# Keeping back the next pair's weight copies in a macaron block: an order edge on ScalarE instead of two one-column writes on VectorE

## The chip, the cores and the metric

The kernel runs on one core of a Trainium2 chip. The core has TensorE (matmuls, PE in the profile, its weight loads PEld), VectorE (DVE), ScalarE (ACT), GpSimd (POOL) and SyncE (SP), which here issues nearly all DMAs. The metric is the device time of one execution in microseconds; the time of a kernel is the median of its runs.

## What is computed

One layer of a macaron block on 1024 frames of 1024 features in float32: half a SwiGLU feed-forward, a stick-breaking attention with 16 heads of 64, and half a second feed-forward, each behind an RMS norm.

```python
x = x + 0.5 * swiglu(rms_norm(x, n1), wi1, wo1)
x = x + stick_breaking_attention(rms_norm(x, gm), w_qkv, gq, gk, w_o)
x = x + 0.5 * swiglu(rms_norm(x, n2), wi2, wo2)

# attention, per head; q and k are RMS-normed per head
z = (q @ k.T) / 8                                # 1024 x 1024, only s < t counts
w[t, s] = sigmoid(z[t, s]) * prod(1 - sigmoid(z[t, j]) for s < j < t)
o = w @ v
```

## The kernel before

Every float32 matmul is made of three: each operand is split into a high part (a copy on ScalarE that rounds to the matmul's type, `hi`) and a low part (the difference, `lo`, by VectorE or GpSimd), and `mm3` (lines 301 to 310) adds hi·hi, hi·lo and lo·hi. `split` (lines 195 to 197) is that pair of instructions, so line 196 is always ScalarE's copy and line 197 the subtraction.

The two feed-forwards lie before and behind the attention stage. The attention stage works through eight pairs of heads, and the change lies there. In one round of 66 us the kernel scores one pair, applies its weights to the values, and computes q, k and v of the next pair. A round has four parts, a to d: the two heads times the two halves of the queries.

- **Scores** (`scores`, lines 1038 to 1073): two matmuls into a bank `bz` (L1058), two sigmoids on ScalarE (L1062; one gives the weight tile `w`, the other overwrites `bz` with 1 - sigmoid), a running product on VectorE (the scan, L1064, into `om` or `w`), and a multiply on GpSimd (L1071).
- **Values** (`values`, lines 1075 to 1130): transposes of `w` into a bank `bt` (L1093), the split into `th` (ScalarE, L196) and `tl` (VectorE, L197), and matmuls into a bank `bo`, first with `th`, then with `tl` (L1111). At the end of a head, `bo` is evacuated (L1116, L1117); the finished pair is split into `w` tiles (`w<-o`, L196 and L197) and stored by DMA (L1125).
- **Projections of the next pair** (`qkv`, lines 956 to 1010): 24 matmuls per block of 128 frames into a bank `bq`, in steps of nine, nine and six; then `bq` is evacuated by ScalarE (`sq`, `qk`, `vst`; L980, L981, L984). After four blocks VectorE computes the reciprocal roots (lines 208 to 212), the rates `r` (L992) and the factors `f` of the sigmoids (L1003), and GpSimd applies `r` to `qk` (L996, L999). `prep_q` and `prep_k` transpose them (L1016) and split them (L1020, L1021).
- **Weights of the pair after the next** (`weights_of`, lines 926 to 954): four steps, k = 0, 2, 4 and 6. Each loads two blocks of `w_qkv` by DMA into `raw_qkv` (L941, two tiles in turn), copies them on ScalarE into the high part `wqh` (L948), and GpSimd subtracts for the low part `wql` (L951). The four steps are put at fixed times of a round (`LOADS`, two in part c, two in part d).

What order the engines work in is decided when the program is built: a scheduler takes the instructions by the plan's order and by their dependencies and puts each engine's queue in order. A copy like L948 depends on its load alone, so it could be queued much earlier than the plan means. The kernel keeps it back by a small write: before the copy, an engine writes two columns (`[:, ks, 0]`, 128x2) of the tile that the copy will fill, from a value that is only known late (`behind`, L944 to L946). The copy overwrites that column, but it can't pass the write. In the rounds of pairs 2 to 7 the first two steps (k = 0 and 2) are held by a VectorE write of `r` into `wqh` and a GpSimd write of `qk` into `wql`; the last two by a GpSimd write into `wqh`.

There is a second means, used at line 947 for pair 1: `tc.issue_after(mark)` tells the scheduler to queue an instruction behind another one, without data between them. `following` (line 192) does the same and does nothing for `None`.

Of the kernel before, what the change touches and what calls it, by code (L numbers as in the profile page):

```python
# [12 lines left out]
AF = mybir.ActivationFunctionType  # L13
# [32 lines left out]
LOADS = (("c", 14.0), ("c", 15.0), ("d", 9.0), ("d", 10.0))  # L46
# [67 lines left out]
def macaron_kernel(ctx, tc, x, g1, w1_in, w1_out, gm, w_qkv, gq, gk, w_o, g2, w2_in, w2_out, out):  # L114
    nc = tc.nc
    act, dve, pool_e, pe, sp = nc.scalar, nc.vector, nc.gpsimd, nc.tensor, nc.sync
# [4 lines left out]
    marks = {}  # L121
# [70 lines left out]
    def following(mark):  # L192
        return tc.issue_after(mark) if mark is not None else nullcontext()
# [472 lines left out]
    with pools(*RAWS) as pr:  # L666
# [3 lines left out]
        with banks("ps1"), pools(*STREAM) as pa:  # L670
            with pools("x") as px, pools("xs", side="right") as pl:
                rows_of = {}

                def load_x(tbs):
# [5 lines left out]
                ss, mean, r = (  # L680
                    pl["xs"].tile([P, NT * n], F32, name=nm, bufs=1) for nm, n in (("ss", 2), ("mean", 1), ("r", 1))
                )
# [184 lines left out]
        with banks("ps2"), pools(*SECOND) as pl:  # L867
            lay_banks()
            gain_m = load_gain(pn, gm)
            half = pn["xs"].tile([P, 4, 2], F32, name="half", bufs=1)  # L870
# [45 lines left out]
    with ExitStack() as stack:  # L916
# [9 lines left out]
        def weights_of(p, state, behind, after=None):  # L926

            wh, wl = state["wq"] = {}, {}

            def step(n, k):
                if k % 4 == 0:
                    wq = pl[f"wq{(2 * p + k // 4) % 4}"]
                    state["h"], state["l"] = (wq.tile([P, 4, 3 * P], F32R, name=f"wq{n}", bufs=1) for n in "hl")
                h_, l_ = state["h"], state["l"]
                raw = pl["raw_qkv"].tile([P, 2, 3, P], F32, name="raw_qkv")
                src = w_qkv[k * P : (k + 2) * P, :].rearrange("(k p) (a c) -> p k a c", p=P, a=3)
                for i in range(2):  # L940
                    state["loaded"] = sp.dma_start(raw[:, i], src[:, i, :, p * P : (p + 1) * P]).ins  # L941
                ks = slice(k % 4, k % 4 + 2)
                raw = raw.rearrange("p k a c -> p k (a c)")
                for engine, to, f in behind[n]:  # L944
                    there = f().to_broadcast([P, 2])
                    engine.tensor_tensor((h_, l_)[to][:, ks, 0], there, there, op=ALU.mult)  # L946
                with tc.issue_after(after[k]) if after and k in after else nullcontext():
                    act.activation(h_[:, ks], raw, AF.Copy)  # L948
                for i in range(2):
                    k_ = k % 4 + i  # L950
                    pool_e.tensor_tensor(l_[:, k_, :], raw[:, i, :], h_[:, k_, :].bitcast(F32), op=ALU.subtract)  # L951
                    wh[k + i], wl[k + i] = h_[:, k % 4 + i, :], l_[:, k % 4 + i, :]

            return [partial(step, i // 2, k) for i, k in enumerate((4, 6, 0, 2) if p == 0 else (0, 2, 4, 6))]
# [83 lines left out]
        def scores(state, hd, half):  # L1038

            w = state["w", hd, half] = {}  # L1040

            def step(tb, kb):
                L = T - tb * P
                if kb == half:
                    t = pl["w"].tile([P, T - tb % 4 * P], F32, name=f"w{hd}{tb % 4}", bufs=1)

                    om = t[:, L : 2 * L] if half else pl["om"].tile([P, T], F32, name="om")
                    state["om"], w[tb] = om, t[:, :L]
                om, wt = state["om"], w[tb]
                q = state["q", hd, half][:, (tb % 4) * P : (tb % 4 + 1) * P]  # L1050
                s0 = max(tb * P, kb * NHALF)
                n = (kb + 1) * NHALF - s0
                c0 = s0 - tb * P
                off = P if n == P else 0
                z = bank("bz")
                keys = slice(s0 - off - kb * NHALF, NHALF)
                for i in range(2):
                    pe.matmul(z[:, : off + n], q, state["k", hd, kb][i][:, keys], start=i == 0, stop=i == 1)  # L1058

                z = z[:, off : off + n]  # L1060
                for to, sign in ((wt[:, c0 : c0 + n], 0), (z, 1)):
                    act.activation(to, z, AF.Sigmoid, scale=state["f", half][:, sign, tb % 4, hd : hd + 1])  # L1062
                least = first[:, P : P + 1].to_broadcast([P, n]) if c0 else first[:, :n]
                dve.tensor_tensor_scan(  # L1064
                    om[:, c0 : c0 + n], z, least, initial=om[:, c0 - 1 : c0] if c0 else 0.0,
                    op0=ALU.mult, op1=ALU.max,
                )
                if c0 == 0:
                    pool_e.memset(wt[:, 0:1], 0.0)
                c1 = max(c0, 1)  # L1070
                pool_e.tensor_tensor(wt[:, c1 : c0 + n], wt[:, c1 : c0 + n], om[:, c1 - 1 : c0 + n - 1], op=ALU.mult)  # L1071

            return [partial(step, tb, kb) for tb in range(half * 4, half * 4 + 4) for kb in range(half, 2)]

        def values(state, p, hd, half):
# [63 lines left out]
        states = [{} for _ in range(NP)]  # L1139
        plan = []  # L1140

        def spread(steps, t0, t1, at=0.5):
            plan.extend((t0 + (t1 - t0) * (i + at) / len(steps), f) for i, f in enumerate(steps))
# [9 lines left out]
                f()  # L1153
        first_q = ((pool_e, 0, lambda: states[0]["qk", 1][:, 0, 0, 0:1]),)
        evacuated = {}
        loads = weights_of(1, states[1], (first_q, first_q), evacuated)
        for i, f in enumerate(steps[:12]):
            f()

# [15 lines left out]
        for p in range(-1, NP):  # L1175
            this = states[p] if p >= 0 else None
            nxt = states[p + 1] if p < NP - 1 else None
            start, t = {}, PAIR * p
            for part, span in PARTS.items():
                start[part], t = t, t + span  # L1180

            def put(part, t, f):
                plan.append((start[part] + t, f))

            for part, span in PARTS.items():
                state = nxt if part == "d" else this
                if state is not None:
                    spread(scores(state, *UNITS[part]), start[part], start[part] + span, 0.5)
                if this is not None:
                    groups = values(this, p, *BEFORE[part])  # L1190
                    for i, (to_turn, to_apply) in enumerate(groups):
                        t = TURN + (span - TURN) * i / len(groups)
                        put(part, t, to_turn)
                        put(part, t + APPLY, to_apply)
            if nxt is not None:
                if p >= 0:
                    fills = qkv(p + 1, nxt)
                    for part, span in PARTS.items():
                        for i in range(FILLS[part]):
                            put(part, (span - (3.0 if part == "d" else 0.0)) * (i + 0.5) / FILLS[part], fills.pop(0))  # L1200
                put("c", 15.0, partial(prep_q, nxt, 1))
                put("c", 17.5 if p >= 0 else 20.0, partial(prep_k, nxt, 0, 1))
                put("d", 8.0, partial(prep_k, nxt, 1, 1))
            if this is not None:
                put("a", 5.0, partial(prep_q, this, 0))
                put("a", 7.5, partial(prep_k, this, 0, 0))
                put("b", 8.0, partial(prep_k, this, 1, 0))
            if 0 <= p < NP - 2:

                held = (  # L1210
                    ((dve, 0, lambda s=nxt: s["r"][:, 0, 0:1]), (pool_e, 1, lambda s=nxt: s["qk", 1][:, 0, 4, 0:1])),
                    ((pool_e, 0, lambda s=nxt: s["qk", 0][:, 2, 0, 0:1]),),
                )
                for at, f in zip(LOADS, weights_of(p + 2, states[p + 2], held)):
                    put(*at, f)
            if p == NP - 2:

                def note(i, f):
                    pool_e.tensor_tensor(seen[:, i : i + 1], f(), f(), op=ALU.mult)

                put("c", 14.0, partial(note, 0, lambda s=nxt: s["qk", 1][:, 0, 4, 0:1]))
                put("d", 1.0, partial(note, 1, lambda s=nxt: s["k", 0, 1][1][:, 0:1].bitcast(F32)))
                put("c", 10.0, partial(load_o, 1))
                put("d", 15.5, lambda: spots.append(tc.cur_priority))
            if p == NP - 1:
                put("a", 2.5, partial(load_o, 0))
                for at, _, _ in SHARES:
                    put(*at, lambda: spots.append(tc.cur_priority))
# [7 lines left out]
    after = ExitStack()  # L1236
# [128 lines left out]
```

## Time and profile before

| what | value |
|---|---|
| runs | 1933.4, 1935.77, 1935.79 us; median 1935.77 |
| profiled execution | 1933.84 us, its span 1932.1 us |
| clock granted to TensorE | full speed in all 40 slices |
| DMA | mean 134 GB/s over the span, about 40 GB/s in the attention rounds |
| VectorE writes at L946 | 12, from 739.9 to 1070.6 us |

The attention stage reaches from about 640 to 1250 us; its full rounds start at 740, 806, 872, 938 and 1004 us and so on. The page lists for each engine its busy time; the chain of waits goes back from the last instruction through whatever released it; the timeline gives single instructions with start and duration in us. A row's brackets hold the idle time of the engine ahead of it and what ended it. Times in the timeline count from the start of the span.

### The profile page before, as it was taken

To read this page: it belongs to the slowest core of one execution; us is meant where nothing else is said; L and a number is where in the kernel's file an instruction comes from. 1 tells how busy PE (TensorE), PEld (TensorE's weight loads), DVE (VectorE), ACT (ScalarE), POOL (GpSimd) and SP (SyncE) were. 2 spreads that over 40 slices of the span, in tenths; PEclk is the share of its full clock that TensorE was granted. 3 is DMA by queue.
4 is the path that set the end of the run, shared out by engine and by line. 5 is a ranking of instruction groups with operands and counts; after the bars stand their busy time and mean duration, and the time that the engine had idled before them with its cause. 6 is when DMAs were issued, how large, how long until landed. Compare 5 with 4: busy or idle time off the path is not lost.

```text
span 1932.1 us, 26665 instructions
## 1 busy us (share of the span) xinstructions
PE 1905.4 (99%) x9362; PEld 1622.9 (84%) x9362; DVE 1243.5 (64%) x1726; ACT 981.8 (51%) x1794; POOL 1115.5 (58%) x994
## 2 busy tenths in 40 slices
PE   9999999999999999999999999999999999999999
PEld 8878888888888898899889897788888888888887
DVE  6855455536775667887787778477555545548645
ACT  6433433444335467777787777344433443334332
POOL 6766667656456645555665664114667667654554
PEclk9999999999999999999999999999999999999999
DMA  6232323238896401111101144511323233369973
GB/s 202 93 120 99 104 88 126 95 123 305 315 341 233 134 17 49 35 39 45 44 31 47 50 135 149 194 57 53 122 88 125 95 102 102 122 216 340 334 264 142
DMA packets 169558, 259.70 MB, mean 134 GB/s; under 512 B 11728, under 2 KB 82384, under 8 KB 169424
## 3 DMA queue, kind: packets, MB, share of 16 engines
q1 hardware_dynamic: 169280, 258.00, 39.1%
q8 instruction: 73, 1.20, 0.3%
q14 instruction: 61, 0.50, 0.1%
q10 hardware_dynamic: 144, 0.00, 0.0%
HBM read 197.66 MB, written 60.29 MB: 134 GB/s over the span
## 4 chain that ended last, share of the span: by engine, by line
PE 84%; DVE 8%; ACT 3%; POOL 2%; issue 2%; DMA 1%; DVEq 0%; POOLq 0%; ACTq 0%
PE ka L308 6%; PE ka L309 6%; PE ka L310 6%; PE kc L309 4%; PE kc L308 4%; PE kc L310 4%; PE ma L310 4%; PE ma L308 4%; PE kb L309 4%; PE kb L308 4%; PE kb L310 4%; PE ma L309 4%; PE bq L308 4%; PE bq L309 4%; PE bq L310 4%; PE mb L310 3%
## 5 line engine op out<-in xcount | busy, mean ns | idle before, releaser
L197 POOL TENSOR_TENSOR rp<-raw,rp 128x1024 fp32r<-128x1024 f32 x84 | 210.2, 2507 | 172.6 <-ACT rp L196 157.0
L197 POOL TENSOR_TENSOR u<-sf,u 128x512 fp32r<-128x512 f32 x160 | 227.6, 1424 | 136.2 <-ACT u L196 136.2
L197 POOL TENSOR_TENSOR u<-raw,u 128x512 fp32r<-128x512 f32 x128 | 186.9, 1462 | 157.3 <-ACT u L196 156.5
L1071 POOL TENSOR_TENSOR w<-w,om 128x512 f32<-128x512 f32 (+4 forms) x128 | 141.1, 1106 | 114.7 <-DVE om L1064 88.5
L196 ACT ACTIVATE u<-sf 128x512 fp32r<-128x512 f32 x160 | 100.8, 630 | 204.7 <-PE kb L309 86.8
L446 DVE TENSOR_TENSOR h<-h 128x512 f32<-128x512 f32 x110 | 135.3, 1234 | 85.8 <-POOL h L554 85.1
L308 PE MATMUL bq<-wqh,xh 128*128 128x384 f32 x512 | 174.6, 341 | 0.0
L196 ACT ACTIVATE rp<-rh 128x1024 fp32r<-128x1024 f32 (+1 forms) x78 | 76.5, 984 | 189.9 <-issue 56.7
L310 PE MATMUL bq<-wqh,xl 128*128 128x384 f32 x512 | 172.2, 336 | 0.0
L309 PE MATMUL bq<-wql,xh 128*128 128x384 f32 x512 | 172.1, 336 | 0.0
L576 DVE TENSOR_TENSOR raw<-raw 128x1024 f32<-128x1024 f32 (+1 forms) x60 | 95.4, 1594 | 106.3 <-DMA raw<-w_out 95.5
L196 ACT ACTIVATE u<-raw 128x512 fp32r<-128x512 f32 x128 | 80.3, 630 | 151.5 <-PE ka L309 100.8
L308 PE MATMUL ka<-xh,u 128*128 128x512 f32 x352 | 137.2, 390 | 1.9 <-ACT s L499 1.9
L308 PE MATMUL ma<-rp 128*128 128x512 f32 x352 | 137.0, 389 | 0.0
L309 PE MATMUL ka<-xl,u 128*128 128x512 f32 x352 | 137.0, 389 | 0.0
L310 PE MATMUL ma<-rp 128*128 128x512 f32 x352 | 136.9, 389 | 0.0
L310 PE MATMUL ka<-xh,u 128*128 128x512 f32 x352 | 136.9, 389 | 0.0
L309 PE MATMUL ma<-rp 128*128 128x512 f32 x352 | 136.9, 389 | 0.0
L1062 ACT ACTIVATE w<-bz,f 128x512 f32<-128x512 f32 (+2 forms) x192 | 112.5, 586 | 40.5 <-PE bz L1058 39.0
L554 POOL TENSOR_TENSOR h<-h,g 128x512 f32<-128x512 f32 x80 | 113.0, 1412 | 34.9 <-DVE h L503 33.0
L475 DVE TENSOR_TENSOR sf<-raw 128x512 f32<-128x512 f32 x80 | 80.2, 1003 | 78.0 <-POOL u L197 78.0
L197 DVE TENSOR_TENSOR rp<-rh,rp 128x1024 fp32r<-128x1024 f32 (+1 forms) x70 | 107.7, 1555 | 22.2 <-ACT rp L196 19.6
(310 smaller groups left out, 5500.9 us busy)
## 6 DMA issues: line engine op xcount, KB each, us to landing
raw<-w_out SPq DMA_DIRECT2D x120, 512.0 KB, 5.5
raw<-w_in SPq DMA_DIRECT2D x86, 512.0 KB, 3.6
k<-h SPq DMA_DIRECT2D x154, 256.0 KB, 2.0
rh<-k SPq DMA_DIRECT2D x64, 512.0 KB, 6.2
raw_qkv<-w_qkv SPq DMA_DIRECT2D x64, 192.0 KB, 2.9
x_keep<-x SPq DMA_DIRECT2D x32, 256.0 KB, 3.7
x<-x_keep SPq DMA_DIRECT2D x32, 256.0 KB, 5.6
raw<-w_out SPq DMA_DIRECT2D x24, 256.0 KB, 4.6
```

The source lines that it names most:

```text
L196: first = act.activation(hi, raw, AF.Copy).ins
L197: return first, (engine or dve).tensor_tensor(lo, raw, hi.bitcast(F32), op=ALU.subtract).ins
L308: pe.matmul(dst, ah, bh, start=start and i == 0, stop=False, skip_group_check=onto)
L309: pe.matmul(dst, ah, bl, start=False, stop=False, skip_group_check=onto)
L310: pe.matmul(dst, al, bh, start=False, stop=stop and i == n - 1, skip_group_check=onto)
L446: dve.tensor_tensor(src, hb[of[0]], hb[of[1]], op=getattr(ALU, of[2]))
L475: dve.tensor_tensor(f[n], x, y, op=op)
L554: pool_e.tensor_tensor(h, h, gs[k], op=ALU.mult)
L576: dve.tensor_tensor(w[0], w[0], w[1], op=getattr(ALU, W_OF[m][2]))
L1062: act.activation(to, z, AF.Sigmoid, scale=state["f", half][:, sign, tb % 4, hd : hd + 1])
L1071: pool_e.tensor_tensor(wt[:, c1 : c0 + n], wt[:, c1 : c0 + n], om[:, c1 - 1 : c0 + n - 1], op=ALU.mult)
```

## The change

`marks["scored"]` now holds the sigmoid that was issued last. For the pairs from the third on, the copies of the steps k = 0 and 2 are queued behind that sigmoid, and VectorE's write of `r` is left out. GpSimd's write into `wql` stays. `after` is now called as a function, so pair 1 passes `evacuated.get` and keeps its edge.

```diff
-                with tc.issue_after(after[k]) if after and k in after else nullcontext():
+                with following(after and after(k)):
                     act.activation(h_[:, ks], raw, AF.Copy)
...
                 for to, sign in ((wt[:, c0 : c0 + n], 0), (z, 1)):
-                    act.activation(to, z, AF.Sigmoid, scale=state["f", half][:, sign, tb % 4, hd : hd + 1])
+                    marks["scored"] = act.activation(
+                        to, z, AF.Sigmoid, scale=state["f", half][:, sign, tb % 4, hd : hd + 1]
+                    ).ins
...
-        loads = weights_of(1, states[1], (first_q, first_q), evacuated)
+        loads = weights_of(1, states[1], (first_q, first_q), evacuated.get)
...
                 held = (
-                    ((dve, 0, lambda s=nxt: s["r"][:, 0, 0:1]), (pool_e, 1, lambda s=nxt: s["qk", 1][:, 0, 4, 0:1])),
+                    ((pool_e, 1, lambda s=nxt: s["qk", 1][:, 0, 4, 0:1]),),
                     ((pool_e, 0, lambda s=nxt: s["qk", 0][:, 2, 0, 0:1]),),
                 )
-                for at, f in zip(LOADS, weights_of(p + 2, states[p + 2], held)):
+                for at, f in zip(LOADS, weights_of(p + 2, states[p + 2], held, lambda k: marks["scored"] if k < 4 else None)):
```

In the built program the queue of VectorE changes in six places, all alike. Here is the first of them, in part c of a round, from the rates `r` of the next pair on; first VectorE's queue of before, with what each instruction waits for:

```order
L992 TENSOR_SCALAR r<-bq 128x4x2 [waits DVE_49]
L1003 TENSOR_SCALAR f_6882<-bq 128x8 x2
L946 TENSOR_TENSOR wqh<-r 128x2 [waits DVE_49]
L946 TENSOR_TENSOR wqh<-r 128x2
L197 TENSOR_TENSOR tl<-bt,th 128x512 [waits Activation_49]
```

and of the changed kernel:

```order
L992 TENSOR_SCALAR r<-bq 128x4x2 [waits DVE_49]
L1003 TENSOR_SCALAR f_6882<-bq 128x8 x2
L197 TENSOR_TENSOR tl<-bt,th 128x512 [waits Activation_49]
L1066 SCALAR_TENSOR_TENSOR om<-bz,first 128x256 [waits Activation_49,Pool_49]
L986 TENSOR_REDUCE ssq<-sq 128x4 [waits Activation_49]
```

The two writes of both steps stood one behind the other, ahead of the subtraction `tl`; they are gone, and `tl` follows the factors `f` at once. (Lines behind 1062 are two higher in the changed kernel.)

On ScalarE at the same place of the round, before:

```order
L1062 ACTIVATE bz<-bz,f_6467 128x256
L948 ACTIVATE wqh<-raw_qkv 128x768 [waits DMAHW2_49,DMAHW1_49,DVE_49]
L980 ACTIVATE sq<-bq 128x256 [waits PE_49]
L981 ACTIVATE qk_6917<-bq 128x256
L984 ACTIVATE vst<-bq 128x2x64
L196 ACTIVATE th<-bt 128x512 [waits PE_49,Activation_49]
```

and of the changed kernel:

```order
L1062 ACTIVATE bz<-bz,f_6467 128x256
L948 ACTIVATE wqh<-raw_qkv 128x768 [waits DMAHW2_49,DMAHW1_49]
L980 ACTIVATE sq<-bq 128x256 [waits PE_49]
L981 ACTIVATE qk_6917<-bq 128x256
L984 ACTIVATE vst<-bq 128x2x64
L196 ACTIVATE th<-bt 128x512 [waits DVE_49,PE_49]
```

No instruction of ScalarE has moved: the copy L948 stands behind the same sigmoid and waits for its load alone. What it no longer waits for, `th` behind it now names itself. The queues of ScalarE, GpSimd, TensorE and SyncE hold the same instructions in the same order in both kernels.

## The prediction

> **What bounds the kernel now.** I read the page first: busy shares, then the chain that ended last.
>
> ```profile
> span 1932.1 us, 26665 instructions
> PE 1905.4 (99%) x9362; PEld 1622.9 (84%) x9362; DVE 1243.5 (64%) x1726; ACT 981.8 (51%) x1794; POOL 1115.5 (58%) x994
> PE 84%; DVE 8%; ACT 3%; POOL 2%; issue 2%; DMA 1%; DVEq 0%; POOLq 0%; ACTq 0%
> ```
>
> TensorE is busy in 1905.4 of 1932.1 us, so all the idle time that any change of waits can remove is 26.7 us. VectorE is 64% busy, but it carries 8% of the chain: in places TensorE waits for it. The change touches six rounds of the attention stage, so the next view is the busy time by stretch, one stretch for each round of 66 us (the columns are PE, weight loads, DVE, ACT and POOL, then the granted clock, the DMA share and GB/s; here the first and the last of five full rounds).
>
> ```profile
> 740.00:806.00 66.00, 64.21 (x389) 59.22 (x389) 52.97 (x104) 51.67 (x113) 38.40 (x59) 1.00 0.13 41
> 1004.00:1070.00 66.00, 64.25 (x390) 59.28 (x390) 53.01 (x103) 51.74 (x113) 38.47 (x59) 1.00 0.13 41
> ```
>
> A round repeats to a few hundredths. Its 66.00 us hold 64.21 us of matmuls at full clock, so TensorE idles 1.8 us per round. The waits of TensorE from 739 to 806 us name them (total, times, longest):
>
> ```profile
> PE bo L1111 <- DVE tl L197: 1.0, 2, 0.8
> PE bt L1093 <- POOL w L1069: 0.6, 1, 0.6
> PE bz L1058 <- DVE w L1064: 0.2, 1, 0.2
> ```
>
> The longest, 0.8 us, is a value matmul that waits for VectorE's subtraction `tl`. The chain, in order of time, shows what stands ahead of that subtraction:
>
> ```profile
> 804.12 1.28 DVE om L1064
> 805.49 0.19 DVE bq L212
> 806.02 0.69 DVE wqh L946
> 806.86 0.61 DVE tl L197
> 807.51 0.50 PE bo L1111
> ```
>
> The writes into `wqh` at line 946 are those that the change removes, and they lie **on** the chain, between VectorE's rate arithmetic and the `tl` that TensorE waits for.
>
> **What the change removes, and its price.** Instruction by instruction in the first round (start, duration; in brackets the idle time before it and its releaser):
>
> ```profile
> L946 DVE TENSOR_TENSOR wqh<-r x12: 149/496/855, 739.9 to 1070.6; 128x2 fp32r<-128x2 f32 x12
> 739.79 0.23 DVE L1003 TENSOR_SCALAR f<-bq 128x8 f32<-128x8 f32 x2
> 739.94 0.85 DVE L946 TENSOR_TENSOR wqh<-r 128x2 fp32r<-128x2 f32 x1
> 739.94 0.92 DVE L946 TENSOR_TENSOR wqh<-r 128x2 fp32r<-128x2 f32 x2
> 740.78 0.68 DVE L197 TENSOR_TENSOR tl<-bt,th 128x512 fp32r<-128x512 f32 x1
> 739.32 0.60 ACT L196 ACTIVATE th<-bt 128x512 fp32r<-128x512 f32 x1 [1.24 <-issue]
> 740.36 0.40 PE L1111 MATMUL bo<-th,vst 128*128 128x512 f32 x1
> 741.51 0.50 PE L1111 MATMUL bo<-tl,vst 128*128 128x512 f32 x1 [0.76 <-DVE tl L197]
> 1071.44 0.50 PE L1111 MATMUL bo<-tl,vst 128*128 128x512 f32 x1 [0.73 <-DVE tl L197]
> ```
>
> Twelve writes, two in each of six rounds, starting from 739.9 to 1070.6 us. They hold VectorE from 739.94 to 740.86. `tl` needs `th`, which ScalarE ends at 739.32 + 0.60 = 739.92. With the writes gone `tl` starts at about 739.96 (0.04 us after `th`) and not at 740.78: **0.82 us earlier**. It ends at 739.96 + 0.68 = 740.64, and TensorE, which started 0.05 us after the end of `tl` before (741.46 to 741.51), starts at 740.69. What else could hold TensorE there?
>
> ```profile
> 738.18 0.39 PE L1111 MATMUL bo<-th,vst 128*128 128x512 f32 x1
> 738.41 0.39 PE L1111 MATMUL bo<-tl,vst 128*128 128x512 f32 x1
> ```
>
> Where the same two matmuls run without a wait they start 0.23 us apart, so TensorE itself would be ready at 740.36 + 0.23 = 740.59. The gain per round is at most 741.51 - 740.59 = 0.92 us, and 0.82 if `th` sets it. The last of the six waits (1071.44) is 0.73 us by the same measure by which the first is 0.76, so I take 0.8 for each round.
>
> Why the first write takes 0.85 us for two columns, when the second takes 0.15 (the least of the twelve is 149 ns), the POOL rows suggest:
>
> ```profile
> 739.48 1.29 POOL L1071 TENSOR_TENSOR w<-w,om 128x512 f32<-128x512 f32 x1 [2.10 <-DVE rs_u L211]
> 744.07 2.95 POOL L951 TENSOR_TENSOR wql<-raw_qkv,wqh 128x384 fp32r<-128x384 f32 x3
> 746.47 0.56 DVE L197 TENSOR_TENSOR tl<-bt,th 128x384 fp32r<-128x384 f32 x1
> ```
>
> GpSimd's multiply ends at 739.48 + 1.29 = 740.77, and the first write at 740.79: it looks as if it had waited for GpSimd. [...] The write has two SBUF inputs; `tl` reads one from PSUM and one from SBUF, and at 746.47 it ran beside GpSimd in 0.56 us, not stretched. So `tl`, put in the place of the write, should not inherit the stall.
>
> [...]
>
> **What the change adds.** The edge on ScalarE. The rows of both orders above show every instruction of ScalarE at its old place: the copy L948 stood right behind a sigmoid before, and does after. An edge behind an instruction that precedes it on the same engine costs nothing. GpSimd, TensorE and the DMA queue keep their orders. So nothing is put in the way of anything; the copy only loses its wait for VectorE.
>
> ```profile
> 740.17 0.45 ACT L1062 ACTIVATE bz<-bz,f 128x256 f32<-128x256 f32 x1
> 740.82 0.84 ACT L948 ACTIVATE wqh<-raw_qkv 128x768 fp32r<-128x768 f32 x1 [0.20 <-DVE wqh L946]
> 746.07 19.40 SPq L941 DMA_DIRECT2D raw_qkv<-w_qkv  x8
> raw_qkv<-w_qkv SPq DMA_DIRECT2D x8, 192.0 KB, 3.0
> ```
>
> It comes 0.2 us earlier, at 740.62. It still waits for its load. A round's eight loads are issued from 746.07 to 765.47 and land 3.0 us later, and the copy that uses the last of them is the one a round later, at 740.82 + 66 = 806.8: no new wait. Queued behind the copy are the evacuation of `bq` and the next `th`, which win those 0.2 us too.
>
> **Does the gain stay?** TensorE comes 0.82 us earlier, ScalarE at first only 0.2, and GpSimd not at all until it next idles. So the question is who is late next.
>
> ```profile
> 742.54 0.60 ACT L196 ACTIVATE th<-bt 128x512 fp32r<-128x512 f32 x1 [0.17 <-PE bt L1093]
> 747.50 0.76 DVE L1021 SCALAR_TENSOR_TENSOR q_s<-bz,gq_sb,q_s 64x512 fp32r<-64x512 f32 x1
> 748.02 0.69 ACT L1020 ACTIVATE kh_s<-bz,gk_sb 128x512 fp32r<-128x512 f32 x1 [0.56 <-PE bz L1016]
> 748.53 0.48 PE L1058 MATMUL bz<-kh_s,q_s 128*128 128x512 f32 x1
> 752.00 1.29 POOL L1071 TENSOR_TENSOR w<-w,om 128x512 f32<-128x512 f32 x1 [2.31 <-DVE om L1064]
> ```
>
> ScalarE's idle 0.17 us at 742.54 waited for TensorE, so its lead grows to at least 0.2 + 0.17 = 0.37 us there. The tightest place that I find is at 748.53: the matmul into a score bank needs VectorE's second `q_s` of that bank (747.50 + 0.76 = 748.26), 0.27 us before. TensorE would come at 748.53 - 0.82 = 747.71, so this `q_s` has to come 0.55 us earlier. VectorE follows ScalarE's copies here. With no more than the lead of 0.37 us a wait of 0.55 - 0.37 = 0.18 us would remain; I expect less, since these copies read what TensorE has just written, and TensorE is early. Behind this place ScalarE idles 0.56 us for TensorE (748.02) and GpSimd 2.31 us (752.00), so both take over the whole lead, and the rest of the round hangs on TensorE. I cost the follow-on at nothing, with 0.2 us per round as its bound.
>
> **Sum.** 6 x 0.8 = 4.8 us. Upper bound 6 x 0.92 = 5.5. Lower bound below nothing only with the last rival. The profiled execution took 1933.84 us (span 1932.1 and 1.7 us around it) and would take 1929.0. It lies 1.9 us under the median of the runs shown, 1935.77 (1933.4 to 1935.79); from the median, 1935.8 - 4.8 = **1931.0 us**. A measurement of this kernel can tell about 0.2%, 3.9 us, from no change: the forecast passes this by 0.9 us only.
>
> **Rivals.**
> - The lead is partly lost: ScalarE's 0.37 us is all that the next stretch takes over. 6 x 0.4 = 2.4 us, 1933.4. For it: ScalarE is busy nearly without a gap from 739 to 747. Against: TensorE waits for none of its results there. Chance 0.15.
> - `tl` inherits the stall, since whatever VectorE runs beside that GpSimd multiply must wait until 740.77. Then only the second write's share goes, 6 x 0.07 = 0.4 us: 1935.4. Against: the unstretched `tl` at 746.47. Chance 0.10.
> - The change doesn't do what it says, and the copy slips ahead or back on ScalarE. Both orders exclude it; 1935.8, chance 0.02.
> - **Slower.** The other VectorE instruction with two SBUF inputs is `w<-o,w`, and it meets a GpSimd multiply once in each round:
>
> ```profile
> 796.36 0.67 DVE L197 TENSOR_TENSOR w<-o,w 128x512 fp32r<-128x512 f32 x1
> 796.52 1.63 POOL L1071 TENSOR_TENSOR w<-w,om 128x512 f32<-128x512 f32 x1 [3.10 <-DVE om L1064]
> ```
>
> VectorE comes first by 0.16 us, and GpSimd takes 1.63 us in place of 1.29. If the new spacing put GpSimd ahead, VectorE would stand until 796.52 + 1.29 = 797.81, 1.45 us later, ahead of scans on the chain: 6 x 1.45 = 8.7 less 4.8, 3.9 us slower, 1939.7. It decides at 0.16 us of relative shift. Against: both hang on the same scan, and move together. Chance 0.03.
>
> **Chances and range.** Forecast 0.70, the rivals 0.15, 0.10, 0.02 and 0.03. The runs shown are 2.4 us apart, so the forecast's own range is 1928.6 (1933.4 - 4.8) to 1932; with the partly lost lead the range ends at 1934. Faster by over 0.2% needs less than 1931.9: 0.70 x 0.8 and a little of the first rival, 0.6. Same 0.36: the rest of these, the second and the third rival. Slower 0.04.
>
> **What the profile would show.** Right: no VectorE instruction at line 946; `tl` starting 0.04 us after `th`; the 0.7 us wait of the value matmul gone in six rounds; rounds of 65.2 us. Wrong: `tl` at its old distance from the GpSimd multiply (second rival), a new wait of a score matmul near 748 us, or a `w<-o,w` of 2 us. What would make it wrong as a whole is a wait that I take to move with TensorE but that hangs on something fixed, such as a transfer in the projection that follows.

## The result, and the profile after

The changed kernel took 1930.83 us (median of 11 runs, 1929.82 to 1931.52), the kernel before in the same session 1935.12 us (11 runs, 1933.4 to 1936.62). The ratio is 0.9978 with a 95% interval of 0.997 to 0.9987: 4.29 us faster, with 2.5 to 5.8 us inside the interval. The forecast was 1931.0 us, and 4.8 us of gain.

The head of the page of the changed kernel, whose profiled execution took 1931.22 us:

```profile
span 1929.4 us, 26653 instructions
PE 1906.1 (99%) x9362; PEld 1623.1 (84%) x9362; DVE 1237.0 (64%) x1714; ACT 978.5 (51%) x1794; POOL 1115.7 (58%) x994
PE 85%; DVE 7%; ACT 2%; POOL 2%; issue 2%; DMA 1%; SPq 0%; DVEq 0%; POOLq 0%; ACTq 0%
```

TensorE does the same work (1906.1 against 1905.4 us busy). VectorE has 12 instructions and 6.5 us less, and its share of the chain falls from 8% to 7%. Next come the stretches, here cut from one calculation of `r` (L992) to the next, so that each row is exactly one round (columns as before: PE, weight loads, DVE, ACT, POOL, granted clock, DMA share, GB/s):

```profile
740.53:805.71 65.18, 64.17 (x390) 59.23 (x389) 52.37 (x101) 51.27 (x113) 38.36 (x59) 1.00 0.13 41
805.71:870.93 65.22, 64.19 (x390) 59.24 (x389) 52.40 (x100) 51.32 (x113) 38.34 (x59) 1.00 0.13 41
870.93:937.29 66.36, 64.40 (x390) 59.19 (x389) 52.57 (x101) 51.28 (x113) 38.42 (x59) 1.00 0.13 41
937.29:1002.50 65.21, 64.16 (x390) 59.23 (x389) 52.38 (x101) 51.27 (x113) 38.35 (x59) 1.00 0.13 41
1002.50:1067.70 65.20, 64.13 (x390) 59.21 (x389) 52.39 (x101) 51.31 (x113) 38.38 (x59) 1.00 0.13 41
```

Four of the five rounds took 65.2 us in place of 66.0, as forecast. The third row is 1.15 us longer than the others, which needs an explanation of its own (below). The waits of TensorE in the first of these rounds, from 739 to 804 us (total, times, longest):

```profile
PE bt L1095 <- POOL w L1071: 0.6, 1, 0.6
PE bo L1113 <- DVE tl L197: 0.2, 1, 0.2
PE bz L1058 <- DVE w L1066: 0.2, 1, 0.2
```

Of the 1.0 us that value matmuls waited for `tl` in two places, the 0.8 at the removed writes is gone. No other wait of TensorE has grown in this round. The timeline at that place (start, duration; in brackets the idle time before it and its releaser):

```profile
740.15 0.60 ACT L196 ACTIVATE th<-bt 128x512 fp32r<-128x512 f32 x1 [1.25 <-issue]
740.30 1.30 POOL L1073 TENSOR_TENSOR w<-w,om 128x512 f32<-128x512 f32 x1 [2.10 <-DVE rs_u L211]
740.61 0.23 DVE L1003 TENSOR_SCALAR f<-bq 128x8 f32<-128x8 f32 x2
740.78 0.69 DVE L197 TENSOR_TENSOR tl<-bt,th 128x512 fp32r<-128x512 f32 x1
741.19 0.40 PE L1113 MATMUL bo<-th,vst 128*128 128x512 f32 x1
741.53 0.50 PE L1113 MATMUL bo<-tl,vst 128*128 128x512 f32 x1
741.36 0.85 ACT L948 ACTIVATE wqh<-raw_qkv 128x768 fp32r<-128x768 f32 x1
748.04 0.69 ACT L1020 ACTIVATE kh_s<-bz,gk_sb 128x512 fp32r<-128x512 f32 x1 [0.56 <-PE bz L1016]
```

`th` ends at 740.15 + 0.60 = 740.75 and `tl` starts at 740.78, 0.03 us behind. VectorE has no idle time ahead of `tl`: it is in `f` until 740.61 + 0.23 = 740.84, so its own queue bounds the start of `tl` too, and not `th` alone. `tl` runs in 0.69 us although GpSimd's multiply is under way until 741.60: the stall did not pass on to it. The matmul with `tl` follows the one with `th` after 0.34 us, where it was 1.15 before: 0.81 us. The copy L948 has no wait, and ScalarE's idle time ahead of `kh_s` (748.04) is 0.56 us as before, so the lead reaches that far.

The round that is too long shows this at its middle. On ScalarE, SyncE and TensorE:

```profile
901.81 0.33 SPq L1127 DMA_DIRECT2D o_keeph<-w  x1
905.59 0.47 ACT L1062 ACTIVATE w<-bz,f 128x256 f32<-128x256 f32 x1 [1.76 <-DMA o_keeph<-w]
907.18 0.39 PE L1058 MATMUL bz<-kh_s,q_s 128*128 128x256 f32 x1 [1.07 <-DVE w L1066]
```

A sigmoid writes into the `w` tile out of which the finished pair is being stored, and waits 1.76 us for that store; the next score matmul then waits 1.07 us. In the profile of before the same sigmoid waited less (the first row is the timeline, the others the view of DMAs from 900 to 908 us: packets, MB and share of the DMA engines' time; then KB and us from issue to landing):

```profile
906.07 0.48 ACT L1062 ACTIVATE w<-bz,f 128x256 f32<-128x256 f32 x1 [0.57 <-DMA o_keeph<-w]
...
q8 instruction: 1, 0.02, 0.7%
...
o_keeph<-w SPq DMA_DIRECT2D x1, 256.0 KB, 2.5
```

and in the changed kernel the same view from 900 to 908 us has

```profile
q8 instruction: 1, 0.02, 1.1%
...
o_keeph<-w SPq DMA_DIRECT2D x1, 256.0 KB, 3.7
```

The store landed after 3.7 us there, after 2.5 us in the profile of before, and after 2.0 us in every other full round of both. One packet of instructions (queue q8, 0.02 MB) passes in this window in both profiles: 1.09 us behind the issue of the store in the changed kernel, 2.00 us behind it in the kernel before. The round of before was not lengthened (66.01 us from `r` to `r`). Numbers 1, 2 and 5 below put VectorE's writes back, and their profiles all have a round that is too long at this place, so the profile of before was a lucky one here, and the two spans, 1932.1 and 1929.4, lie only 2.7 us apart.

### The profile page after: what moved, and what is told of

It is laid out like the page before. It is cut to its first block, busy times and chain, and to the rows that moved or that the text cites. A ratio compares the mean times of both kernels' runs of the same rounds, so it can differ in the third digit from the quotient of the medians.

```text
span 1929.4 us, 26653 instructions
## 1 busy us (share of the span) xinstructions
PE 1906.1 (99%) x9362; PEld 1623.1 (84%) x9362; DVE 1237.0 (64%) x1714; ACT 978.5 (51%) x1794; POOL 1115.7 (58%) x994
## 4 chain that ended last, share of the span: by engine, by line
PE 85%; DVE 7%; ACT 2%; POOL 2%; issue 2%; DMA 1%; SPq 0%; DVEq 0%; POOLq 0%; ACTq 0%
PE ka L308 6%; PE ka L310 6%; PE ka L309 6%; PE kc L308 4%; PE kc L310 4%; PE kc L309 4%; PE bq L309 4%; PE bq L308 4%; PE bq L310 4%; PE kb L308 4%; PE ma L309 4%; PE ma L310 4%; PE kb L310 4%; PE ma L308 4%; PE kb L309 4%; PE bo L1113 3%
## 5 line engine op out<-in xcount | busy, mean ns | idle before, releaser
L576 DVE TENSOR_TENSOR raw<-raw 128x1024 f32<-128x1024 f32 (+1 forms) x60 | 89.9, 1500 | 109.8 <-DMA raw<-w_out 94.9
```

The costliest lines, as they stand in the source:

```text
L576: dve.tensor_tensor(w[0], w[0], w[1], op=getattr(ALU, W_OF[m][2]))
```

## The experiments

All kernels start from the changed one. Of the longer edits only the lines that matter are shown, and `...` marks what is left out. Each was timed beside the kernel before on the same chip; the median of that was 1935.72 us in the first group (the first four), 1936.15 in the second (the next four), 1935.86 and 1935.78 in the last two.

**1. The writes put back, the edge kept.** Is it the edge or the writes?

```diff
-                    ((pool_e, 1, lambda s=nxt: s["qk", 1][:, 0, 4, 0:1]),),
+                    ((dve, 0, lambda s=nxt: s["r"][:, 0, 0:1]), (pool_e, 1, lambda s=nxt: s["qk", 1][:, 0, 4, 0:1])),
```

> The changed kernel with VectorE's two writes per round put back, the edge kept. If the writes cost and the edge is free: the time of the kernel before (about 1935.1 us), rounds of 66.0 us, the value matmul bo<-tl again 1.1 us behind bo<-th. If it is the edge that brings the gain: the time of the changed kernel, 1930.8.

1935.39 us, ratio to before 0.9998 [0.9989, 1.0007]. TensorE's waits from 640 to 1110 us, with the write's row in the list of groups (busy us, mean ns):

```profile
PE bo L1113 <- DVE tl L197: 6.1, 12, 0.7
...
L946 DVE TENSOR_TENSOR wqh<-r 128x2 fp32r<-128x2 f32 x12 | 5.5, 500 | 0.0
```

The wait for `tl` is back at 6.1 us (1.7 in the changed kernel), with the edge in place. The gain belongs to the writes, and the edge has no cost that this comparison shows.

**2. One write only** (put back as in number 1, but for step k = 0 alone).

```diff
                 for engine, to, f in behind[n]:
+                    if engine is dve and k:
+                        continue
```

> The changed kernel with only the first of VectorE's two writes (step k = 0) put back. If the first write waits for the end of GpSimd's multiply: it still takes 0.85 us, tl starts 0.07 us earlier than before, and nearly the whole gain goes: 1930.8 + 6 x 0.73 = 1935.2 less noise, rounds of 65.9 us. If each write costs alike, half the gain stays: 1933, rounds of 65.6 us.

1935.12 us, 0.9997 [0.9988, 1.0006]. The summary of the write's line (least, median and greatest ns, first and last start), and the first round's timeline:

```profile
L948 DVE TENSOR_TENSOR wqh<-r x6: 839/851/858, 739.9 to 1070.6; 128x2 fp32r<-128x2 f32 x6
739.41 1.29 POOL L1075 TENSOR_TENSOR w<-w,om 128x512 f32<-128x512 f32 x1 [2.11 <-DVE rs_u L211]
739.87 0.84 DVE L948 TENSOR_TENSOR wqh<-r 128x2 fp32r<-128x2 f32 x1
740.64 0.68 DVE L197 TENSOR_TENSOR tl<-bt,th 128x512 fp32r<-128x512 f32 x1
```

All six take 0.85 us, and the write ends at 740.71, when GpSimd's multiply does (740.70). In the four profiles that have such a first write from SBUF (before and numbers 1, 2 and 5) it ends 0.02 us behind GpSimd's multiply in each of the six rounds, 24 times in all. Half of the writes cost all of the time: the price is one wait for GpSimd, not a price per write.

**3. Both writes put back, with one of their two inputs read from PSUM** (a value of the same age that lies in `bq`).

```diff
-                    engine.tensor_tensor((h_, l_)[to][:, ks, 0], there, there, op=ALU.mult)
+                    first_in = there
+                    if engine is dve:
+                        first_in = state_y()[:, 0, 2:3].to_broadcast([P, 2])
+                    engine.tensor_tensor((h_, l_)[to][:, ks, 0], first_in, there, op=ALU.mult)
...
```

> Both writes put back, but with one input from PSUM (the rates before they are copied) and one from SBUF, so that no instruction of VectorE there has two SBUF inputs. If two SBUF inputs beside GpSimd's multiply make the stall: each write takes 0.15 to 0.25 us, tl comes about 0.25 us later than in the changed kernel, 1930.8 + 6 x 0.25 = 1932.3 us. If a write takes its 0.85 us for any other reason (its wait for r, its output in wqh): 1935 us. On TensorE the scheduler puts one transpose ahead of bo<-tl in each round, worth 0.1 us at most.

1930.68 us, 0.9973 [0.9964, 0.9983]: the time of the changed kernel and not the 1932.3 of the expectation, with as many VectorE instructions as before. The line's summary and the first round's timeline on GpSimd, VectorE and TensorE:

```profile
L949 DVE TENSOR_TENSOR wqh<-bq,r x12: 148/149/152, 740.1 to 1067.8; 128x2 fp32r<-128x2 f32 x12
739.60 1.29 POOL L1077 TENSOR_TENSOR w<-w,om 128x512 f32<-128x512 f32 x1 [2.11 <-DVE rs_u L211]
740.06 0.21 DVE L949 TENSOR_TENSOR wqh<-bq,r 128x2 fp32r<-128x2 f32 x2
740.49 0.39 PE L1117 MATMUL bo<-th,vst 128*128 128x512 f32 x1
740.72 0.27 PE L1099 MATMUL bt<-ident,w 128*128 128x128 f32 x1
740.92 0.50 PE L1117 MATMUL bo<-tl,vst 128*128 128x512 f32 x1
```

Each write now takes 149 ns under the same multiply, with the same output and the same wait for `r`. So neither the output nor that wait makes the stall, and with one of its two inputs in PSUM the write does not have it. What the two writes still cost does not show in the time. The scheduler put a transpose between the two value matmuls, and it probably covers them.

**4. No hold at all on the copies of k = 0 and 2**: neither write nor edge.

```diff
-                for at, f in zip(LOADS, weights_of(p + 2, states[p + 2], held, lambda k: marks["scored"] if k < 4 else None)):
+                for at, f in zip(LOADS, weights_of(p + 2, states[p + 2], held)):
```

> The changed kernel without the edge: nothing on ScalarE holds the copies of the steps k = 0 and 2. In its order the copies stand earlier, and the scheduler lays out the rounds anew. If the hold matters: slower than the changed kernel by 2 to 10 us, since a copy of 0.85 us stands ahead of sigmoids or splits that TensorE waits for. If only the missing writes matter: 1931 us.

1948.94 us, 1.0068 [1.0054, 1.0082]: 18 us slower than with the edge, far more than the 2 to 10 us that were expected. Waits from 640 to 1110 us, of TensorE and (third row) of ScalarE:

```profile
PE bo L1113 <- ACT th L196: 15.6, 5, 3.2
PE bz L1016 <- POOL qk L996: 4.5, 5, 1.0
...
ACT wqh L948 <- DMA raw_qkv<-w_qkv: 16.9, 12, 2.5
```

The copies are queued so early that ScalarE stands in front of them until their loads land (16.9 us), and `th` and with it TensorE wait behind. So a hold is needed here; the question was only which kind.

**5. Both writes put back as an instruction with one input and a constant** (SBUF to SBUF).

```diff
+                    if engine is dve:
+                        dve.tensor_scalar((h_, l_)[to][:, ks, 0], there, 1.0, None, op0=ALU.mult)
+                    else:
+                        engine.tensor_tensor((h_, l_)[to][:, ks, 0], there, there, op=ALU.mult)
...
```

> Both writes put back as tensor_scalar: one input, in SBUF, and the output in SBUF. If only two SBUF inputs make the stall: writes of 0.1 to 0.2 us and the time of the changed kernel, 1930.8. [...]

1936.06 us, 1.0 [0.9991, 1.0008]. The line's summary:

```profile
L947 DVE TENSOR_SCALAR wqh<-r x12: 154/503/861, 740.6 to 1072.9; 128x2 fp32r<-128x2 f32 x12
```

One input is no way out: the first of two still takes 0.86 us, and the time is not the 1930.8 us of the expectation. So two SBUF inputs are not the whole condition. With both inputs in SBUF the first write takes 0.85 us (number 2), with one of two in PSUM 0.15 (number 3), and with its only input in SBUF 0.86. Why the place of the inputs decides, no run shows.

**6. The next wait attacked**: the split of the finished pair, `w<-o`, is put later for the second half of the queries, so that it is out of the way of GpSimd's multiply, whose `w` the transposes `bt` wait for (3.7 us in all).

```diff
-                    split(o, oh, ol)
-                    for to, src in zip(o_keep, (oh, ol)):
-                        sp.dma_start(to[rows(p), HALVES[half]], src.bitcast(F32))
+                    def keep_o():
+                        split(o, oh, ol)
+                        for to, src in zip(o_keep, (oh, ol)):
+                            sp.dma_start(to[rows(p), HALVES[half]], src.bitcast(F32))
...
+            if 0 <= p < NP - 1:
+                put("c", 4.0, lambda s=this: s["keep_o"]())
```

> The changed kernel, with the split of a finished pair (w<-o on ScalarE and VectorE, for the half that ends in part b) put 4 time units into part c. VectorE's w<-o has two SBUF inputs and stands beside a GpSimd multiply that takes 1.63 us there and 1.29 elsewhere, and TensorE waits 0.6 us for that multiply in each round. If the same exclusion is at work: that multiply takes 1.29 us, TensorE's wait for it falls by 0.34 us, and seven rounds give 2.4 us, 1928.4. If the exclusion only moves on to the next multiply or the wait is set by something else: 1930.8.

1931.64 us, 0.9978 [0.9968, 0.9987]: no gain over the changed kernel. TensorE's wait from 640 to 1110 us, three rows of the first round, and this round by busy time:

```profile
PE bt L1095 <- POOL w L1073: 1.6, 6, 0.3
...
796.27 0.83 DVE L197 TENSOR_TENSOR w<-o,w 128x512 fp32r<-128x512 f32 x1
796.51 1.74 POOL L1073 TENSOR_TENSOR w<-w,om 128x511 f32<-128x511 f32 x1
799.45 0.19 PEld L1113 LDWEIGHTS bo<-tl,vst 128*128 128x128 f32 x1 [0.41 <-DVE tl L197]
...
739.25:804.46 65.21, 64.44 (x390) 59.27 (x389) 52.49 (x101) 51.23 (x113) 38.47 (x59) 1.00 0.13 41
```

The wait fell from 3.7 to 1.6 us, but the round is still 65.21 us. The split only meets other multiplies of GpSimd, and what the expectation calls an exclusion shows as longer times: the split takes 0.83 us in place of 0.67, and the multiply that starts beside it 1.74 in place of 1.29. Matmul by matmul against a round of the changed kernel, TensorE comes 0.32 us earlier out of the wait for GpSimd and has lost this lead 2.9 us later, at the value matmul of 799.45, whose weights wait 0.41 us for VectorE's `tl`. A second wait stood behind the first. This matmul is drawn as 0.50 us in place of 0.40, so that the wait counts as busy time of TensorE, which rose by 0.27 us at the same 390 matmuls.

**7. GpSimd's two writes into `wql` left out as well.**

```diff
-                    ((pool_e, 1, lambda s=nxt: s["qk", 1][:, 0, 4, 0:1]),),
+                    (),
```

> The changed kernel without GpSimd's two writes into wql for the steps k = 0 and 2 either; the order of all else stays. GpSimd is idle for 1.5 us at the end of that stretch (before its multiply at 752), so its 0.35 us per round are hidden: 1930.8. If GpSimd is what is late behind the change: up to 6 x 0.35 = 2.1 us faster, 1928.7.

1931.21 us, 0.9975 [0.9965, 0.9985]: like the changed kernel. The same kind of write costs nothing that shows on an engine that has time there: in the first round of the changed kernel the two take 0.35 us of GpSimd from 743.30, and GpSimd idles for 1.51 us ahead of its multiply at 752.01.

**8. All four steps held by edges, no writes at all.**

```diff
-                for at, f in zip(LOADS, weights_of(p + 2, states[p + 2], held, lambda k: marks["scored"] if k < 4 else None)):
+                held = ((), ())
+                for at, f in zip(LOADS, weights_of(p + 2, states[p + 2], held, lambda k: marks["scored"])):
...
```

> All four steps held by the edge on ScalarE and no writes at all. The copies of the steps k = 4 and 6 then stand elsewhere (one later by a matmul bank's worth of work), and the scheduler changes the order of several instructions of TensorE. If a hold by an edge is free wherever it stands: 1930.8 or a little less. If the place in the order decides: slower by 1 to 6 us, 1932 to 1937.

1930.23 us, 0.9971 [0.9959, 0.9982]. The undisturbed rounds took 64.7 us (739.85 to 804.52 and on to 869.18), 0.5 less than with two edges, but a value matmul lost 1.9 us at one place of the last stretch, from 1068 to 1140 us:

```profile
PE bo L1113 <- ACT th L196: 1.9, 1, 1.9
```

**9. The same for every pair but the last**, which is held as in the changed kernel.

```diff
+                last = p == NP - 3
...
+                    ((pool_e, 1, lambda s=nxt: s["qk", 1][:, 0, 4, 0:1]),) if last else (),
+                    ((pool_e, 0, lambda s=nxt: s["qk", 0][:, 2, 0, 0:1]),) if last else (),
...
+                for at, f in zip(LOADS, weights_of(p + 2, states[p + 2], held, lambda k, last=last: marks["scored"] if k < 4 or not last else None)):
```

> All four steps of weight copies are held by the edge behind the sigmoid issued last, for every pair but the last; the last pair is held as in the changed kernel (edge for two steps, GpSimd's writes kept). Theory (the 0.55 us per round that the four edges won were given back in the last stretch only because the last pair's copies stood differently there): the five rounds keep about 65.2 - 0.55 us, the stretch from 1098 us on takes its old time, and the kernel takes 1930.8 - 2.5 = 1928.3 us. Rival (the rounds' shorter time is only work pushed to the end, whatever holds the last pair): 1930 to 1931 us, as with four edges everywhere, with the last stretch again some 2.5 us longer.

**10. The changed kernel once more**, beside number 9.

> The changed kernel itself, on the same chip as the run beside it, to compare the two directly: 1930.8 us by every theory, within 1929.8 to 1931.6. Its fourth round (871 to 937 us) should again be longer than 65.2 us by 1 to 2 us, with ScalarE's sigmoid waiting for the store of the finished pair, if that stall is a standing part of the kernel; 65.2 us if it comes by chance.

Number 9 took 1929.19 us (1927.44 to 1929.51), 0.9962 [0.9948, 0.9975], number 10 1930.72 us (1930.38 to 1932.39), 0.9976 [0.9966, 0.9985]. The 1.9-us wait is gone, and 1.5 us of the 2.5 that were expected came. Number 9 is the fastest of all by its median, though the two intervals overlap. Both show the long round: from `r` to `r` number 9 has 66.34 us (868.68 to 935.02) where the round before has 64.71, number 10 has 66.74 (869.91 to 936.65) beside 65.19. The gain of the change itself can be read from numbers 1 and 10, since number 1 is the old kernel's work and has the long round too (67.28 us, 871.44 to 938.72). From the first `r` to that of the half round after the sixth write, number 1 needs 739.45 to 1104.09, 364.64 us, and number 10 739.53 to 1099.70, 360.17: **4.47 us** less.

**11. The instruction fetches moved.** TensorE has 2 x 9362 instructions (matmuls and weight loads) and the page of the changed kernel lists

```profile
q8 instruction: 73, 1.20, 0.3%
```

These are 73 packets of 16.4 KB, one for 256.5 instructions of TensorE. In the profile of the changed kernel TensorE starts 210 to 301 instructions from one packet to the next, 254 in the mean, so I take them for the fetches of its instructions. A round has 780 of TensorE's instructions, three times 256.5 and about 10 more, so by this count one of the fetches comes about 1 us earlier against the round each time; in the profile of the changed kernel the steps are 1.1 to 2.1 us. In the round from 870.93 us on (the expectations call it the fourth) it passes while the store is on its way. Splitting nine of the 18 empty warm-up matmuls at the kernel's start into two halves each adds 18 instructions ahead of everything without adding columns, and so should move all fetches ahead by 1.5 us (780 instructions in 65.2 us are 12 per us).

```diff
-                for _ in range(IDLE):
-                    go("pe", lambda: pe.matmul(idle, zeros[:, :P], zeros, start=True, stop=True))
+                for n in [NHALF] * (IDLE - 9) + [NHALF // 2] * 18:
+                    go("pe", lambda: pe.matmul(idle[:, :n], zeros[:, :P], zeros[:, :n], start=True, stop=True))
```

> The changed kernel, and in TensorE's idle start nine of its 18 empty warm-up matmuls of 512 columns are each two of 256: the same columns, 18 instructions (nine matmuls, nine weight loads) more ahead of everything else on TensorE. In the profiles an instruction fetch of 0.02 MB comes once per 256 TensorE instructions, and a round has 780, so that one of them moves by about 1 us per round against the store of the finished pair: 3.5, 2.6, 0.9 us behind the issue of the store, then 1.2 and 2.3 us ahead of it, and the 0.9 is the fourth round, whose sigmoid waits. Theory (the fetch on top of the store makes it land late): 18 instructions move every fetch 1.5 us ahead, so the store of the round from 805 us on is now the one that takes 3 to 4 us and that round is 66.2 to 66.7 us, while the round from 871 us on falls to 65.2. Rival (the fourth store is late for another reason): the fourth round stays 1 to 2 us too long. The time is 1930.8 us within 0.5 by both.

**12. The kernel of number 9 with the fetches moved 72 instructions ahead.** As number 11, with 12 of the 18 cut into four.

> The kernel with four edges for every pair but the last, and 12 of the 18 warm-up matmuls are each four of 128 columns: 72 instructions more ahead on TensorE, which move every fetch 6 us ahead. Theory (the fetch makes the store late): it then lies 1 us or more ahead of the store in every full round, no sigmoid waits for a store, all five full rounds are 64.65 us, and the kernel takes 1929.2 - 1.5 = 1927.7 us. Rival (another reason): the fourth round stays at 66.3 us and the time at 1929.2.

Number 11 took 1932.54 us (0.998 [0.9972, 0.9989]). Its rounds, cut as above, and the two sigmoids that waited:

```profile
740.29:807.28 66.99, 64.43 (x390) 59.22 (x389) 52.56 (x101) 51.30 (x113) 38.42 (x59) 1.00 0.13 40
807.28:873.51 66.23, 64.42 (x390) 59.17 (x390) 52.58 (x101) 51.27 (x113) 38.39 (x59) 1.00 0.13 41
873.51:938.72 65.21, 64.17 (x390) 59.25 (x390) 52.40 (x101) 51.27 (x113) 38.35 (x59) 1.00 0.13 42
...
775.60 0.47 ACT L1062 ACTIVATE w<-bz,f 128x256 f32<-128x256 f32 x1 [2.35 <-DMA o_keeph<-w]
841.82 0.48 ACT L1062 ACTIVATE w<-bz,f 128x256 f32<-128x256 f32 x1 [1.62 <-DMA o_keeph<-w]
```

The stall left the round in which it had stood in every profile of this kernel and moved to earlier ones, as the theory said. It said one round, and it was two: the store of the round from 740 us on, which I had put out of reach, landed late too (4.3 and 3.5 us, then 2.0 in the other three). The fetches had moved by 0.2 to 2.6 us against the stores of the five rounds, and not by 1.5 in each, so the instruction count alone does not set their times. The two rounds are 1.79 and 1.03 us longer than 65.2, together 2.82, where number 10 loses 1.55: that is 1.3 of the 1.8 us by which this kernel is slower than number 10. The time was expected to stay within 0.5 us of 1930.8, and missed that.

Number 12 had no such stall: all five stores landed in 2.0 us, no sigmoid waited longer than 0.2 us for one, and all five full rounds took 64.6 to 64.7 us. Here are two of them, and the warm-up matmuls of number 12 and of number 9:

```profile
811.39:876.06 64.67, 63.85 (x390) 59.14 (x390) 52.12 (x101) 51.55 (x113) 38.21 (x55) 1.00 0.13 42
876.06:940.70 64.64, 63.83 (x390) 59.12 (x389) 52.11 (x101) 51.40 (x113) 38.20 (x55) 1.00 0.13 42
...
1.64 13.06 PE L691 MATMUL kc<-xl 128*128 128x512 f32 x54 [1.64 <-POOL xl L685]
...
1.64 6.26 PE L691 MATMUL kc<-xl 128*128 128x512 f32 x18 [1.64 <-POOL xl L685]
```

But its median is 1931.02 us, not 1927.7. In this profile the 54 warm-up matmuls took 13.06 us, where the 18 of number 9 with the same columns took 6.26, and the first matmul of the feed-forward came at 17.17 us, there at 9.87. Its six runs fall in two groups, 1927.56 to 1929.02 and 1933.01 to 1933.23, and the profile is one of the second. What separates them was not found, and whether the runs of the first group have the long warm-up too is not known.

The other profiles fit the theory as well. In all 14 of this document, between 700 and 1080 us, a fetch passed 0.85 to 1.17 us behind the issue of an `o_keeph` store thirteen times, and each of these stores landed after 3.3 to 4.4 us. The other `o_keeph` stores landed after 2.0 to 2.5 us, but for one in number 6 (the fetch 1.90 us behind, 4.3 us). With numbers 11 and 12 this shows that the fetch makes the store late; how to gain time from it is not shown.

## Why the prediction was right, point by point

- **Where the time was.** The wait of the value matmul for `tl` stood on the chain, and it went in all six rounds. This is confirmed, and tied to the writes by experiment 1.
- **0.82 us per round.** `tl` was to start 0.04 us behind `th`, and started 0.03 behind; the two matmuls stand 0.34 us apart, the bound by TensorE itself was 0.23. Rounds of 65.2 us came out to the digit. The prediction named `th` alone as what `tl` would wait for; VectorE's own queue, with `f` until 740.84, sets nearly the same moment, so that this step came out does not show that `th` sets it.
- **6 x 0.8 = 4.8 us.** Measured 4.29 between the medians, and 4.47 between two profiles that both have the late store. The stall is not quite the same: the long round loses 66.74 - 65.19 = 1.55 us in number 10 and 67.28 - 65.98 = 1.30 in number 1. With that, 4.47 + 0.25 = 4.72 us, and 0.79 per round. That the time itself (1931.0 against 1930.83) agrees to 0.2 us is in part luck: the forecast started from 1935.8, 0.7 us above the 1935.12 measured beside the changed kernel, and its gain was 0.5 us above the 4.29 measured.
- **The start from the median.** The shown profile, 1933.84 us, less 4.8 would have given 1929.0, and the profile of the changed kernel took 1931.2. Of the 2.2 us, 1.15 are the late store and 0.82 the later start of the first round (`r` at 740.53 against 739.71); the rest is the rounding of 0.8 and what lies around the span. The median most likely holds the late store: the profiles with the writes that show it took 1935.03, 1934.55 and 1936.08 us (numbers 1, 2 and 5), and the one without it 1933.84. So it was the better base; the prediction chose it without knowing this reason, which is luck.
- **The cause of the 0.85 us.** The row suggested a wait for GpSimd; that the write's two SBUF inputs make it wait, no row of before shows. The wait is now supported three ways: the write ends with the multiply (number 2, 740.71 beside 740.70), an input from PSUM takes the stall away (number 3, 0.15 us), and a single SBUF input does not (number 5, 0.86 us). Number 5 also shows that two SBUF inputs, by which the prediction told the write from `tl`, are not the only case. No run took the multiply itself away.
- **The follow-on at nothing.** Right: there is no new wait near 748 us, where the second `q_s` ends 0.21 us before the score matmul starts, and four of five rounds keep 0.8 us. The rival of a partly lost lead falls.
- **The edge at nothing.** Right, as far as experiment 1 can tell (ratio 0.9989 to 1.0007). But the hold itself is worth 18 us (experiment 4), which the prediction had no need to price.
- **`tl` inherits the stall.** This rival falls: `tl` took 0.69 us under the multiply. The slower rival, `w<-o,w` behind GpSimd, did not occur either: it still starts 0.16 us ahead of the multiply and takes 0.67 us.
- **What it overlooked.** It did not see the store out of the `w` tile and the sigmoid behind it, and told of transfers only as a general risk. The late store costs about the same with the writes and without (1.30 us in number 1, 1.55 in number 10), so the difference stood.

## What to carry to other kernels

A dummy write that only orders work is an instruction like any other. It can take on the wait for a big one on a neighbouring engine: here a write of 128x2 elements took 0.85 us, and the two writes of a round cost 0.8 us of the chain, six times. An order edge on the engine that issues the held work was free here, where it moved no instruction (number 1: 1935.39 us with edge and writes, 1935.72 with the writes alone). A write that reads from PSUM (number 3: 0.15 us each, 1930.68 us), or one on an engine with time to spare (number 7: 1931.21 us without it, 1930.83 with it), cost nothing that showed either. And before a small gain is taken from two single profiles, look for a stall that one of them lacks by luck.

## What the runs showed of the hardware that was not expected

- One fetch of 16.4 KB, taken for one of TensorE's instructions, passing about 1 us behind the issue of a 256-KB store, made that store land after 3.3 to 4.4 us in place of 2.0. The fetch wanders against the store (from 3.7 us behind its issue to 2.1 ahead over the five rounds of the changed kernel), as the 780 instructions of a round are not a multiple of 256.5, the number per fetch, and 18 more instructions at the start of the kernel moved the stall to other rounds (number 11). How the two get in each other's way, no run shows.
- A warm-up burst of the same columns took 5.8 to 7.2 us in the twelve profiles with 18 matmuls, 7.2 in the one with 27 and 13.1 in the one with 54.
